# Up-projections of three feed-forward stages as seven products of summed quarters, down-projections in five interleaved groups

## The chip, the cores and the metric

The kernel runs on one core of a Trainium2 chip. The metric is the device time of one execution in microseconds, the median of several runs. One further execution was taken with the hardware profiler; its span, from the first to the last instruction, and its own time stand below.

## The reference, cut to what matters

All tensors are float32. There are 512 tokens, the model width is 1024, the feed-forward width 2816. A first block (mixer, convolutional feed-forward, gate) is followed by two layers, each of them a feed-forward stage, attention and another feed-forward stage:

```python
def swiglu(h, wg, wu, wd):
    return (jax.nn.silu(h @ wg) * (h @ wu)) @ wd

for i in range(DEPTH_2):          # DEPTH_2 = 2
    x = x + 0.5 * swiglu(rmsnorm_2(x, ffn_norm1[i]), ffn1_wg[i], ffn1_wu[i], ffn1_wd[i])
    h = rmsnorm_2(x, mix_norm[i])
    ...                           # i = 0: sliding-window attention, i = 1: latent attention
    x = x + 0.5 * swiglu(rmsnorm_2(x, ffn_norm2[i]), ffn2_wg[i], ffn2_wu[i], ffn2_wd[i])
```

The change touches three of these four stages: the second of layer 0 (f20 below), the first of layer 1 (f11) and the second of layer 1 (f21). f20 and f11 follow each other directly.

## The kernel before

Activations lie transposed: the residual x is eight tiles of 128 features by 512 tokens. Every float32 number that goes into TensorE is split into a high part, rounded to the type fp32r, and the rest; `mm` then makes three matmuls of one product: high by high, high by rest, rest by high. Weights come from one flat array, in the order of their use, in chunks of 128 by 1024 (eight blocks of 128 by 128). `Weights` loads a chunk (tile `wr`), rounds it on ScalarE (`wh`) and subtracts on VectorE (`wl`), up to four chunks ahead.

A stage (`ffn`, `swiglu`, `up_down`) works in this order. Of the 22 blocks of 128 hidden features, twelve are made by `pair(j)`: one chunk for the gate and one for the up-projection, each eight blocks of `mm` into one PSUM bank (24 matmuls of 512 columns), multiplied by the token norms `rB` on VectorE, SiLU on ScalarE, the product of both, and its split. Then `down(0)` sums eleven hidden blocks into each of the eight output tiles and adds them to x. Ten more pairs follow, and `down(1)`. Before a stage's first product can be scaled, `operands` splits x times its gain, and `rstd_tok` and `bcast` make the norms.

The order of instructions on every engine isn't the program's text: calls are recorded by `Order`, and `arrange` lays them out ahead of time by costs, due times and free buffers. A buffer pool has a fixed number of slots; PSUM has five banks for `ps` and three for `pt`. All recorded instructions come out of one line (`Order.emit`), which is why every row of the profile has the same line number.

Of the kernel before, what the change touches and what calls it, by code (L numbers as in the profile page):

```python
# [20 lines left out]
P = 128  # L21
S = 512
D = 1024
KD = D // P
# [5 lines left out]
CH = 1024  # L30
AHEAD = 3
# [7 lines left out]
FEED = (3, 3) + (2,) * 9 + (0,) * 5  # L39
AHEAD_OF = 200  # L40
URGENCY = (0.0, 0.5)
SPARE = {"f": 3, "ps": 3, "e": 2}

# [90 lines left out]
def pack_ffn(which, i):  # L134
    def f(a):
        return pack_up_down(a[f"ffn{which}_wg_2"][i], a[f"ffn{which}_wu_2"][i], a[f"ffn{which}_wd_2"][i])
    return f


def pack_out(w):  # L140
# [230 lines left out]
class Order:  # L371
# [137 lines left out]
    def _arrange(self, strict):  # L509
# [28 lines left out]
        def fits(o):  # L538
# [112 lines left out]

class Weights:
    def __init__(self, nc, pool, flat, sizes):
        self.nc, self.pool, self.flat, self.sizes = nc, pool, flat, sizes
        self.off = 0
        self.made = 0
        self.used = 0
        self.ready = {}

    def _make(self, parts=1):  # L660
        nc, i = self.nc, self.made
        n = self.sizes[i]
        raw = self.pool.tile([P, CH], F32, name="wr", tag="wr", bufs=3)[:, :n]
        h = self.pool.tile([P, CH], F32R, name="wh", tag="wh", bufs=AHEAD + 1)[:, :n]
        lo = self.pool.tile([P, CH], F32R, name="wl", tag="wl", bufs=AHEAD + 1)[:, :n]
        src = self.flat[self.off:self.off + P * n].rearrange("(p n) -> p n", p=P)
        def piece(c):
            nc.sync.dma_start(out=raw[:, c], in_=src[:, c])
            nc.scalar.copy(out=h[:, c], in_=raw[:, c])
            nc.vector.tensor_tensor(out=lo[:, c], in0=raw[:, c], in1=h[:, c].bitcast(F32), op=ALU.subtract)  # L670

        step = n // parts
        todo = [lambda o=o: piece(slice(o, o + step)) for o in range(0, n, step)]
        self.ready[i] = (h, lo)
        self.off += P * n
        self.made += 1
        return todo


    def first(self):  # L680
        return self._make(4)

    def next(self, n):
        while self.made < len(self.sizes) and self.made <= self.used + AHEAD:
            for piece in self._make():
                piece()
        assert self.sizes[self.used] == n, (self.used, self.sizes[self.used], n)
        r = self.ready.pop(self.used)
        self.used += 1
        return r  # L690


class Core:
    def __init__(self, ctx, tc, A, sizes, vo, co):
        self.tc, self.A = tc, A
        self.nc = nc = Order(tc.nc)

        def pool(name, bufs, space=None):
            kw = {} if space is None else {"space": space}
            return LazyPool(ctx.enter_context(tc.tile_pool(name=name, bufs=bufs, **kw)), bufs, space)  # L700

        self.cp = pool("c", 1)
        self.xp = pool("x", 1)
        self.wp = pool("w", 1)
# [11 lines left out]
        self.W = Weights(nc, self.wp, A["w"], sizes)  # L716
        self.bg = []

    def start(self, x_in):
# [24 lines left out]
    def f(self, n=S):  # L744
        return self.fp.tile([P, FW], F32, name="f", tag="f", bufs=12)[:, :n]
# [32 lines left out]
                self.bg.pop(0)()  # L778


    def mm(self, ps, w, x, start, stop):
        te = self.nc.tensor
        te.matmul(ps, lhsT=w[0], rhs=x[0], start=start, stop=False)
        te.matmul(ps, lhsT=w[0], rhs=x[1], start=False, stop=False)
        te.matmul(ps, lhsT=w[1], rhs=x[0], start=False, stop=stop)

    def proj(self, ops, w, o=0, ps=None):
        ps = ps if ps is not None else self.ps()
# [307 lines left out]
        self.swiglu(xo, rB)  # L1096

    def ffn(self, name):
        xo = self.operands(self.v(name, 0, KD))
        rB = self.bcast(self.rstd_tok())  # L1100
        self.swiglu(xo, rB)

    def swiglu(self, xo, rB):
        nc, W = self.nc, self.W

        def pair(j):
            ps = self.proj(xo, W.next(CH))
            g = self.mul(self.f(), ps, rB)
            nc.scalar.activation(out=g, in_=g, func=AF.Silu)
            ps = self.proj(xo, W.next(CH))  # L1110
            u = self.mul(self.f(), ps, rB)
            self.mul(g, g, u)
            return self.split(g)

        self.up_down(pair, 0.5)

# [556 lines left out]
    (pack_ffn(2, 0), lambda c: c.ffn("f20")),  # L1673
    (pack_ffn(1, 1), lambda c: c.ffn("f11")),
    (pack_attn_b, lambda c: c.attn_b()),
    (pack_ffn(2, 1), lambda c: c.ffn("f21")),
]


def layout(a, phases):  # L1680
    vo, vec = pack_vecs(a)
    co, con = pack_consts()
    arrays = pack_misc(a)
    chunks = [ch for pk, _ in phases for ch in pk(a)]
    arrays["vec"] = np.ascontiguousarray(vec)
    arrays["con"] = con
    flat = np.empty(sum(ch.size for ch in chunks), np.float32)
# [5 lines left out]
    return arrays, vo, co, [ch.shape[1] for ch in chunks]  # L1693


def body(tc, A, phases, sizes, vo, co):
# [27 lines left out]
```

## Time and profile before

| | |
|---|---|
| median of 3 runs | 2680.9 us (2680.84 to 2681.42) |
| profiled execution | 2680.98 us, span 2679.2 us |
| mean granted TensorE clock | 0.995 |
| busy: TensorE / weight loads / VectorE / ScalarE | 2653.8 / 2173.9 / 1529.4 / 957.5 us |

Busy time is the union of an engine's instruction intervals. A matmul's interval is longer than its turn on TensorE, because matmuls are pipelined, so the rate is read from the distance between the starts of matmuls that follow each other. A row of VectorE or ScalarE also lasts a little longer than the distance to the next one's start.

### The profile page before, as it was taken

The numbers are of one execution on the slowest core, as the hardware profiler recorded it, in microseconds if no ns is written. First come the engines' busy times: TensorE is split into PE (matmuls) and PEld (weight loads), VectorE is DVE, ScalarE is ACT, GpSimd is POOL, SyncE is SP. The second block draws the span as 40 slices with busy tenths as digits, with TensorE's granted clock in tenths as the row PEclk, the third lists the DMA queues.
The fourth block names the chain that finished last, engine by engine and source line by source line (L and its number), as shares of the span: only waits on it lengthen the run. The fifth ranks groups of instructions, "written<-read, shape, count | busy, mean of one in ns | idle before, by whom it ended". The sixth has DMA issues, their size and how long they took to land. (4 is left out here: it accounts for less than half of the span.)

```text
span 2679.2 us, 32322 instructions
## 1 busy us (share of the span) xinstructions
PE 2653.8 (99%) x12788; PEld 2173.9 (81%) x12788; DVE 1529.4 (57%) x2665; ACT 957.5 (36%) x1487; POOL 120.8 (5%) x193
## 2 busy tenths in 40 slices
PE   9999999999999999999999999999999899999999
PEld 7888888888887888889788888888888766788887
DVE  7526469969858654447664344544344776644342
ACT  4333244323444222235543223322223574432231
POOL 1100000000000000002300000000000142000000
PEclk9999999999999999999999999999999999999999
DMA  5322232333323422324132222222232100323222
GB/s 173 102 95 87 95 100 95 111 117 106 111 92 96 118 95 96 101 87 131 56 107 99 98 95 97 98 97 94 95 102 91 54 17 28 99 94 99 98 94 79
DMA packets 103015, 254.28 MB, mean 95 GB/s; under 512 B 37376, under 2 KB 39296, under 8 KB 102864
## 3 DMA queue, kind: packets, MB, share of 16 engines
q1 hardware_dynamic: 102560, 251.31, 29.0%
q8 instruction: 100, 1.64, 0.2%
q0 software_dynamic: 304, 0.92, 0.1%
q14 instruction: 51, 0.42, 0.0%
HBM read 242.76 MB, written 9.44 MB: 94 GB/s over the span
## 5 line engine op out<-in xcount | busy, mean ns | idle before, releaser
L646 PE MATMUL ps<-op,wh 128*128 128x512 f32 x6624 | 2053.1, 391 | 6.2 <-DVE f L646 3.5
L646 PEld LDWEIGHTS ps<-op,wh 128*128 128x128 f32 x6624 | 1241.6, 188 | 268.5 <-issue 8.1
L646 PE MATMUL ps<-op,wl 128*128 128x512 f32 x3312 | 1292.5, 390 | 0.0
L646 ACT CAST wh<-wr 128x1024 fp32r<-128x1024 f32 (+3 forms) x471 | 469.0, 996 | 1204.6 <-PE ps L646 741.2
L646 PEld LDWEIGHTS ps<-op,wl 128*128 128x128 f32 x3312 | 622.5, 188 | 130.4 <-issue 0.9
L646 DVE TENSOR_TENSOR wl<-wr,wh 128x1024 fp32r<-128x1024 f32 (+3 forms) x471 | 547.2, 1163 | 308.5 <-ACT wh L646 306.6
L646 DVE TENSOR_TENSOR f<-ps,f 128x512 f32<-128x512 f32 x260 | 178.9, 690 | 434.9 <-PE ps L646 431.4
L646 ACT CAST op<-f 128x512 fp32r<-128x512 f32 x136 | 84.2, 621 | 227.4 <-DVE f L646 227.1
L646 DVE TENSOR_TENSOR f<-f 128x512 f32<-128x512 f32 x213 | 147.3, 692 | 27.6 <-ACT f L646 21.4
L646 PE MATMUL ps<-wh,op 128*128 128x256 f32 (+3 forms) x608 | 149.7, 333 | 4.1 <-ACT opf L646 3.4
L646 DVE TENSOR_TENSOR op<-f,op 128x512 fp32r<-128x512 f32 x136 | 93.7, 691 | 67.1 <-ACT op L646 67.0
L646 PEld LDWEIGHTS ps<-wh,op 128*128 128x128 f32 x608 | 105.9, 194 | 12.5 <-ACT opf L646 3.7
L646 ACT ACTIVATE f<-f 128x512 f32<-128x512 f32 x142 | 89.1, 627 | 45.4 <-DVE f L646 45.3
L646 PE MATMUL ps<-wl,op 128*128 128x256 f32 (+3 forms) x304 | 100.1, 329 | 0.0
L646 DVE SCALAR_TENSOR_TENSOR x<-ps,x 128x512 f32<-128x512 f32 (+1 forms) x68 | 44.4, 657 | 93.3 <-PE ps L646 93.3
L646 ACT ACTIVATE f<-x 128x512 f32<-128x512 f32 x80 | 49.3, 628 | 78.1 <-DVE x L646 77.9
L646 DVE TENSOR_TENSOR x<-ps,x 128x512 f32<-128x512 f32 (+1 forms) x57 | 38.7, 680 | 53.8 <-PE ps L646 53.8
L646 DVE SCALAR_TENSOR_TENSOR f<-f,vec 128x512 f32<-128x512 f32 x88 | 64.7, 747 | 1.1 <-ACT f L646 0.9
L646 PEld LDWEIGHTS ps<-wl,op 128*128 128x128 f32 x304 | 58.9, 194 | 3.2 <-issue 0.2
L646 PE MATMUL pt<-con,opf 128*128 128x128 f32 (+1 forms) x348 | 52.9, 279 | 4.2 <-POOL opf L646 2.1
L646 DVE SCALAR_TENSOR_TENSOR op<-x,vec,op 128x512 fp32r<-128x512 f32 x64 | 47.7, 749 | 9.9 <-ACT op L646 9.9
L646 PEld LDWEIGHTS pt<-con,opf 128*128 128x128 f32 (+1 forms) x348 | 38.5, 135 | 16.6 <-issue 4.8
(181 smaller groups left out, 1277.9 us busy)
## 6 DMA issues: line engine op xcount, KB each, us to landing
wr<-in_w SPq DMA_DIRECT2D x411, 512.0 KB, 3.3
wr<-in_w SPq DMA_DIRECT2D x40, 256.0 KB, 2.6
bias<-e SPq DMA_DIRECT2D x28, 256.0 KB, 3.3
opf<-bias SPq DMA_DIRECT2D x16, 448.0 KB, 6.4
x<-in_xT SPq DMA_DIRECT2D x8, 256.0 KB, 4.7
out_y<-x SPq DMA_DIRECT2D x7, 256.0 KB, 2.0
wr<-in_w SPq DMA_DIRECT2D x4, 416.0 KB, 3.1
wr<-in_w SPq DMA_DIRECT2D x12, 128.0 KB, 2.0
```

Of the source, the lines that this page charges most:

```text
L646: getattr(getattr(self.nc, o.eng), o.name)(*[real(a) for a in o.args], **{k: real(v) for k, v in o.kw.items()})
```

## The change

In the three stages, four of the 22 hidden blocks are still made by pairs. The other eighteen are made two at a time, in nine calls of `block(j)`. The weights of two hidden blocks (gate and up, 512 output features) times 1024 input features by 512 tokens are cut into two halves in every direction, and the four quarter products are formed out of seven products of sums of quarters. A product has half the input blocks (four), two of the four feature blocks, and 256 tokens: 24 matmuls of 256 columns into the halves of one PSUM bank. Sums of products that several results share are left in the bank and the next product is added on top (banks b1, b0, b2); what has to be added besides is added by VectorE. The sums of weight quarters (`_sums`) are made on VectorE from the loaded chunks, and all seven are split as other weights are. The sums of activation quarters (`halves`) are made once a stage. `down` no longer runs twice over eleven hidden blocks, but five times over groups of 4, 4, 4, 4 and 6, in parts of four output tiles that stand between the blocks. Weight tiles share one pool of 34 slots with the operands, where there were 22 for operands and eleven for weights.

```diff
+GROUPS = [range(0, 4), range(4, 8), range(8, 12), range(12, 16), range(16, 22)]
...
+def fast_order():
+    out = [("down", 0, range(0, 4))]
+    for g in range(1, len(GROUPS)):
+        js = list(GROUPS[g][::2])
+        if g == 1:
+            out += [("block", js[0]), ("down", 0, range(4, 8)), ("block", js[1])]
+            continue
+        for n, j in enumerate(js):
+            out.append(("block", j))
+            if n < 2:
+                out.append(("down", g - 1, range(4 * n, 4 * n + 4)))
+    return out + [("down", len(GROUPS) - 1, range(0, 8))]
...
+        def s2():
+            st["21"], st["22"] = self._load(CH), self._load(CH)
+            st["s1"] = self._tile("ws", CH)
+            nc.vector.tensor_tensor(out=st["s1"], in0=st["21"], in1=st["22"], op=ALU.add)
+            st["11"] = self._load(CH)
+            st["s2"] = self._tile("ws", CH)
+            minus(st["s2"], st["s1"], st["11"])
+            return self._split(st["s2"])
...
+        def s3():
+            minus(st["21"], st["11"], st["21"])
+            return self._split(st["21"])
...
+        def s4():
+            minus(st["s2"], st["12"], st["s2"])
+            return self._split(st["s2"])
+
+        return [s2, a11, s3, s1, a12, a22, s4]
...
-        self.opp = pool("op", 22)
+        self.opp = pool("op", 34)
...
+    def halves(self, gain, rB):
...
+        for k in range(4):
+            X = self.opf().rearrange("p (a n) -> p a n", a=2)
+            for a in range(2):
+                j = k + 4 * a
+                nc.vector.scalar_tensor_tensor(out=X[:, a], in0=self.x[j], scalar=gain[:, j:j + 1], in1=rB,
+                                               op0=ALU.mult, op1=ALU.mult)
...
+            part(X[:, :, :H], t[:, 0], t[:, 1])
...
+            part(X[:, 1, H:], last[:, k % 2, 0], last[:, k % 2, 1])
...
+            nc.vector.tensor_tensor(out=T[:, 0:2], in0=X[:, :, H:], in1=X[:, 0].rearrange("p (a n) -> p a n", a=2),
+                                    op=ALU.subtract)
+            nc.vector.tensor_tensor(out=T[:, 2], in0=X[:, 1, H:], in1=T[:, 0], op=ALU.subtract)
+            nc.vector.tensor_tensor(out=T[:, 3], in0=X[:, 1, :H], in1=T[:, 2], op=ALU.subtract)
...
+            part(T, h, lo)
...
+        def block(j):
+            def prod(ps, right, start=False):
+                w = W.next(CH)
+                for a in range(2):
+                    for k in range(4):
+                        self.mm(ps[:, a * H:(a + 1) * H], self.wsl(w, a * 512 + k * P, P), B[right][k],
+                                start and a == k == 0, k == 3,
+                                skip_group_check=True)
...
+            b1, b0, b2 = self.ps(), self.ps(), self.ps()
+            prod(b1, "t2", start=True)
+            prod(b0, "b11", start=True)
+            p1 = self.f()
+            nc.scalar.copy(out=p1, in_=b0)
+            prod(b2, "t3", start=True)
+            u2 = plus(self.f(), b1, p1)
+            prod(b1, "t1")
+            u4 = plus(self.f(), b1, p1)
+            low = self.opf()
+            plus(low[:, S:], b2, u4)
+            prod(b0, "b21")
+            prod(b2, "t4")
+            plus(low[:, :S], b2, u2)
+            prod(b1, "b22")
+            c12 = plus(self.f(), b1, p1)
...
```

Three places show what `arrange` makes of it. The rows are in the order of an engine's queue; names carry buffer numbers, and a row ends with the engines or DMA queues whose semaphores it waits for. `op` is an operand's high and rest, `th` and `tl` are those of a sum of activation quarters, `bb` those of a plain quarter, `ws` a sum of weight quarters.

The first place is TensorE in the middle of stage f20. Before, at the passage from one bank to the next:

```order
L646 MATMUL ps_11713<-op_11351,wl_11612 128x512
L646 MATMUL ps_11713<-op_11373,wh_11603 128x512 x2
L646 MATMUL ps_11713<-op_11373,wl_11612 128x512
L646 MATMUL ps_11747<-op_11195,wh_11640 128x512 [waits Activation_49]
L646 MATMUL ps_11747<-op_11195,wh_11640 128x512
L646 MATMUL ps_11747<-op_11195,wl_11649 128x512 [waits DVE_49]
```

Now, in block 10, where the product into b2 (`ps_12729`) ends and the second product into b1 (`ps_12670`) begins:

```order
L691 MATMUL ps_12729<-th_11683,wh_12630 128x256
L691 MATMUL ps_12729<-tl_11693,wh_12630 128x256
L691 MATMUL ps_12729<-th_11683,wl_12640 128x256
L691 MATMUL ps_12670<-th_11523,wh_12642 128x256 [waits DVE_49]
L691 MATMUL ps_12670<-tl_11532,wh_12642 128x256
L691 MATMUL ps_12670<-th_11523,wl_12649 128x256
```

The matmuls are half as wide, and the first one into b1 waits for VectorE, which must have read b1.

The second place is VectorE in the same stage. Before, the six rows of one pair and the next pair's first:

```order
L646 TENSOR_TENSOR f_11715<-ps_11676,f_11441 128x512 [waits PE_49]
L646 TENSOR_TENSOR wl_11720<-wr_11620,wh_11711 128x1024 [waits DMAHW3_49,Activation_49]
L646 TENSOR_TENSOR f_11749<-ps_11713,f_11441 128x512 [waits PE_49]
L646 TENSOR_TENSOR wl_11754<-wr_11657,wh_11745 128x1024 [waits DMAHW4_49,Activation_49]
L646 TENSOR_TENSOR f_11715<-f_11715,f_11749 128x512 [waits DVE_49]
L646 TENSOR_TENSOR op_11767<-f_11715,op_11767 128x512 [waits Activation_49]
L646 TENSOR_TENSOR f_11786<-ps_11747,f_11441 128x512 [waits PE_49]
```

Now, in block 10, the last split of its weights, then u2 (`f_12741`), u4 (`f_12794`) and the lower results (`opf_12802`), with the next weights and their first sums among them:

```order
L691 TENSOR_TENSOR wl_12710<-ws_12548,wh_12699 128x1024 [waits DVE_49,Activation_49]
L691 TENSOR_TENSOR f_12741<-ps_12670,f_12734 128x512 [waits Activation_49]
L691 TENSOR_TENSOR f_12794<-ps_12670,f_12734 128x512 [waits PE_49]
L691 TENSOR_TENSOR opf_12802<-ps_12729,f_12794 128x512 [waits DVE_49]
L691 TENSOR_TENSOR wl_12809<-wr_12731,wh_12788 128x1024 [waits DMAHW5_49,Activation_49]
L691 TENSOR_TENSOR wl_12823<-wr_12760,wh_12811 128x1024 [waits DMAHW6_49,DVE_49,Activation_49]
L691 TENSOR_TENSOR ws_12836<-wr_12763,wr_12791 128x1024 [waits DMAHW7_49,DMAHW0_49,PE_49]
L691 TENSOR_TENSOR f_12828<-f_12828,ps_12702 128x256 [waits Activation_49]
L691 TENSOR_TENSOR opf_12802<-ps_12729,f_12741 128x512 [waits PE_49]
L691 TENSOR_TENSOR f_12866<-f_12866,opf_12802 128x512 [waits Activation_49]
L691 TENSOR_TENSOR ws_12880<-ws_12836,wr_12838 128x1024 [waits DMAHW1_49]
L691 TENSOR_TENSOR wr_12763<-wr_12838,wr_12763 128x1024
```

For a block, seven weight splits and four weight sums now stand in VectorE's queue among the additions that a later product waits for; the last of the block's own splits (`wl_12710`) stands ahead of u2.

The third place is VectorE at the beginning of f20, now, where the last pairs are finished, the first weight sums are made and the first block's products become possible:

```order
L691 TENSOR_TENSOR tl_11693<-tt_11658,th_11683 128x1024 [waits PE_49,Activation_49]
L691 TENSOR_TENSOR op_11697<-f_11546,op_11697 128x512 [waits Activation_49]
L691 TENSOR_TENSOR op_11702<-f_11620,op_11702 128x512 [waits Activation_49]
L691 TENSOR_TENSOR wl_11712<-wr_11391,wh_11464 128x1024 [waits DMAHW0_49,PE_49]
L691 TENSOR_TENSOR f_11719<-ps_11654,f_11458 128x512
L691 TENSOR_TENSOR ws_11727<-wr_11395,wr_11397 128x1024 [waits DMAHW2_49,DMAHW1_49,PE_49]
L691 TENSOR_TENSOR ws_11738<-ws_11727,wr_11399 128x1024 [waits DMAHW3_49,DVE_49,PE_49]
L691 TENSOR_TENSOR f_11750<-ps_11695,f_11458 128x512 [waits PE_49]
L691 TENSOR_TENSOR wr_11395<-wr_11399,wr_11395 128x1024
L691 TENSOR_TENSOR f_11719<-f_11719,f_11750 128x512 [waits DVE_49,Activation_49]
L691 TENSOR_TENSOR wl_11767<-ws_11738,wh_11754 128x1024 [waits Activation_49]
```

Nothing of this stood here before: the last activation sum (`tl_11693`), two sums and a difference of weight quarters, and the split of the first of them (`wl_11767`), for which the first block's first product waits.

## Rows read from the trace of the kernel before

**Rows 1.** The page: span, busy times, engines and clock in 40 slices.

```profile
span 2679.2 us, 32322 instructions
...
PE 2653.8 (99%) x12788; PEld 2173.9 (81%) x12788; DVE 1529.4 (57%) x2665; ACT 957.5 (36%) x1487; POOL 120.8 (5%) x193
```

**Rows 2.** Busy time and granted clock in stages f20, f11 and f21.

```profile
core 0: us, PE busy (x) PEld busy (x) DVE busy (x) ACT busy (x) POOL busy (x), PEclk, DMA share, GB/s
1369.18:1730.34 361.16, 361.13 (x1595) 298.49 (x1594) 164.41 (x204) 106.67 (x129) 0.00 (x0) 1.00 0.30 98
1730.34:2091.37 361.03, 361.03 (x1595) 298.49 (x1594) 162.72 (x202) 104.64 (x127) 0.00 (x0) 1.00 0.29 94
2313.88:2675.26 361.38, 361.38 (x1595) 298.32 (x1593) 152.30 (x188) 94.85 (x112) 0.00 (x0) 1.00 0.29 94
```

**Rows 3.** Waits in stage f20: who for whom, us in total, times, longest.

```profile
ACT wh L646 <- PE ps L646: 101.8, 36, 4.4
DVE f L646 <- PE ps L646: 101.7, 43, 3.4
...
PEld ps L646 <- issue: 0.5, 2, 0.2
```

**Rows 4.** Timeline of f20, TensorE: start us, duration us; 18 matmuls apart.

```profile
1520.00 0.39 PE L646 MATMUL ps<-op,wl 128*128 128x512 f32 x1
...
1524.08 0.39 PE L646 MATMUL ps<-op,wl 128*128 128x512 f32 x1
```

**Rows 5.** Timeline of the sliding-window attention, TensorE: 138 matmuls apart.

```profile
1212.78 0.40 PE L646 MATMUL ps<-wh,op 128*128 128x256 f32 x2
...
1229.34 0.29 PE L646 MATMUL ps<-wh,op 128*128 128x256 f32 x1
```

**Rows 6.** Groups by shape, 1212.4 to 1229.4 us: count, busy us, mean ns.

```profile
L646 PE MATMUL ps<-wh,op 128*128 128x256 f32 x94 | 17.2, 284 | 0.0
L646 PEld LDWEIGHTS ps<-wh,op 128*128 128x128 f32 x93 | 14.5, 192 | 0.0
L646 PE MATMUL ps<-wl,op 128*128 128x256 f32 x47 | 13.4, 285 | 0.0
```

**Rows 7.** Groups by shape in f20, 1400 to 1700 us.

```profile
L646 DVE TENSOR_TENSOR wl<-wr,wh 128x1024 fp32r<-128x1024 f32 x56 | 68.6, 1225 | 46.6 <-ACT wh L646 46.6
L646 ACT CAST wh<-wr 128x1024 fp32r<-128x1024 f32 x55 | 57.9, 1053 | 168.8 <-PE ps L646 89.3 <-issue 79.5
L646 DVE TENSOR_TENSOR f<-ps,f 128x512 f32<-128x512 f32 x39 | 27.0, 692 | 93.4 <-PE ps L646 93.4
L646 ACT ACTIVATE f<-f 128x512 f32<-128x512 f32 x20 | 12.5, 625 | 0.0
L646 DVE SCALAR_TENSOR_TENSOR x<-ps,x 128x512 f32<-128x512 f32 x11 | 7.6, 688 | 11.9 <-PE ps L646 11.9
```

**Rows 8.** Groups by shape over the span: VectorE and ScalarE, other shapes.

```profile
L646 DVE SCALAR_TENSOR_TENSOR f<-f,vec 128x512 f32<-128x512 f32 x88 | 64.7, 747 | 1.1 <-ACT f L646 0.9
L646 DVE TENSOR_TENSOR wl<-wr,wh 128x256 fp32r<-128x256 f32 x12 | 5.0, 421 | 2.8 <-ACT wh L646 2.8
...
L646 ACT COPY f<-ps 128x512 f32<-128x512 f32 x8 | 4.6, 577 | 0.0
L646 ACT CAST wh<-wr 128x256 fp32r<-128x256 f32 x12 | 4.7, 393 | 4.7 <-issue 3.2 <-DMA wr<-in_w 0.8 <-PE ps L646 0.6
```

**Rows 9.** Timeline of f20: VectorE's first product, and how work is handed over.

```profile
1379.33 0.69 DVE L646 TENSOR_TENSOR f<-ps,f 128x512 f32<-128x512 f32 x1 [0.84 <-ACT f L646]
...
1383.29 1.23 DVE L646 TENSOR_TENSOR wl<-wr,wh 128x1024 fp32r<-128x1024 f32 x1 [0.21 <-ACT wh L646]
1384.43 0.69 DVE L646 TENSOR_TENSOR f<-f 128x512 f32<-128x512 f32 x1
...
1392.84 0.39 PE L646 MATMUL ps<-op,wl 128*128 128x512 f32 x1
...
1393.08 1.05 ACT L646 CAST wh<-wr 128x1024 fp32r<-128x1024 f32 x1 [3.86 <-issue]
1393.26 0.69 DVE L646 TENSOR_TENSOR f<-ps,f 128x512 f32<-128x512 f32 x1 [3.31 <-PE ps L646]
...
1394.17 1.23 DVE L646 TENSOR_TENSOR wl<-wr,wh 128x1024 fp32r<-128x1024 f32 x1 [0.21 <-ACT wh L646]
```

**Rows 10.** TensorE in the attention ahead of f20: waits, then the granted clock.

```profile
1265.94 0.33 PE L646 MATMUL pt<-con,opf 128*128 128x128 f32 x1 [0.98 <-POOL opf L646]
1267.36 0.96 PE L646 MATMUL pt<-con,opf 128*128 128x128 f32 x6 [1.09 <-POOL opf L646]
...
1264.00:1268.00 4.00, 1.93 (x16) 1.00 0.04 11
1268.02:1274.84 6.82, 5.94 (x18) 0.50 0.19 56
```

More of the change, by code (lines that the diff above doesn't have):

```diff
@@ L137, in pack_ffn, with pack_fast, f, down @@
     return f
+GROUPS = [range(0, 4), range(4, 8), range(8, 12), range(12, 16), range(16, 22)]
+def pack_fast(which, i):
+    def f(a):
+        wg, wu, wd = (a[f"ffn{which}_w{c}_2"][i] for c in "gud")
+        out = []
+        def block(j):
+            out.append([_cat([b for w in (wg, wu) for b in _blocks(w, range(4 * half, 4 * half + 4), t * P, (t + 1) * P)])
+                        for t, half in ((j + 1, 0), (j + 1, 1), (j, 0), (j, 1))])
+        def down(g, ms):
+            bl = [b for m in ms for b in _blocks(wd, GROUPS[g], m * P, (m + 1) * P)]
+            for n in range(0, len(bl), 8):
+                out.append(_cat(bl[n:n + 8]))
+        for j in GROUPS[0]:
+            for w in (wg, wu):
+                out.append(_cat(_blocks(w, range(KD), j * P, (j + 1) * P)))
+        for step in fast_order():
+            if step[0] == "block":
+                block(step[1])
+            else:
+                down(step[1], step[2])
+        return out
+    return f
+def fast_order():
[10 more added lines that the diff above has]
+    return out + [("down", len(GROUPS) - 1, range(0, 8))]
 def pack_out(w):
@@ L653, in __init__ @@
     def __init__(self, nc, pool, flat, sizes):
-        self.nc, self.pool, self.flat, self.sizes = nc, pool, flat, sizes
+        self.nc, self.pool, self.flat = nc, pool, flat
         self.off = 0
-        self.made = 0
         self.used = 0
[L658 to L666, printed above, removed]
-        def piece(c):
[L668 to L677, printed above, removed]
@@ L680, in first @@
-    def first(self):
-        return self._make(4)
-    def next(self, n):
[L684 to L689, printed above, removed]
+        self.todo = []
+        for n in sizes:
+            if n:
+                self.todo.append((n, lambda n=n: self._split(self._load(n))))
+            else:
+                self.todo += [(CH, f) for f in self._sums()]
@@ new lines, in __init__, with _tile, _from, _load @@
+        self.ready = []
+    def _tile(self, name, n, dt=F32):
+        return self.pool.tile([P, CH], dt, name=name, tag="op")[:, :n]
+    def _from(self, n):
+        self.off += P * n
+        return self.flat[self.off - P * n:self.off].rearrange("(p n) -> p n", p=P)
+    def _load(self, n):
+        raw = self._tile("wr", n)
+        self.nc.sync.dma_start(out=raw, in_=self._from(n))
+        return raw
+    def _split(self, raw):
+        n = raw.shape[1]
+        h, lo = self._tile("wh", n, F32R), self._tile("wl", n, F32R)
+        self._parts(raw, h, lo)
+        return h, lo
@@ new lines, in _parts, with _sums, minus, a11 @@
+    def _parts(self, raw, h, lo):
+        self.nc.scalar.copy(out=h, in_=raw)
+        self.nc.vector.tensor_tensor(out=lo, in0=raw, in1=h.bitcast(F32), op=ALU.subtract)
+    def _sums(self):
+        nc, st = self.nc, {}
+        def minus(out, a, b):
+            nc.vector.tensor_tensor(out=out, in0=a, in1=b, op=ALU.subtract)
+        def s2():
[6 more added lines that the diff above has]
+            return self._split(st["s2"])
+        def a11():
+            return self._split(st["11"])
+        def s3():
+            minus(st["21"], st["11"], st["21"])
+            return self._split(st["21"])
+        def s1():
+            return self._split(st["s1"])
+        def a12():
+            st["12"] = self._load(CH)
+            return self._split(st["12"])
+        def a22():
+            return self._split(st["22"])
+        def s4():
+            minus(st["s2"], st["12"], st["s2"])
+            return self._split(st["s2"])
+        return [s2, a11, s3, s1, a12, a22, s4]
@@ new lines, in first @@
+    def first(self):
+        n, _ = self.todo.pop(0)
+        raw, h, lo = self._tile("wr", n), self._tile("wh", n, F32R), self._tile("wl", n, F32R)
+        src = self._from(n)
+        self.ready.append((n, (h, lo)))
+        def piece(c):
+            self.nc.sync.dma_start(out=raw[:, c], in_=src[:, c])
+            self._parts(raw[:, c], h[:, c], lo[:, c])
+        return [lambda o=o: piece(slice(o, o + n // 4)) for o in range(0, n, n // 4)]
+    def next(self, n):
+        while self.todo and len(self.ready) <= AHEAD:
+            m, f = self.todo.pop(0)
+            self.ready.append((m, f()))
+        m, r = self.ready.pop(0)
+        assert m == n, (m, n)
@@ L778, in step, with mm @@
                 self.bg.pop(0)()
[L781 removed]
+    def mm(self, ps, w, x, start, stop, **kw):
         te = self.nc.tensor
[L783 to L785 removed]
+        te.matmul(ps, lhsT=w[0], rhs=x[0], start=start, stop=False, **kw)
+        te.matmul(ps, lhsT=w[0], rhs=x[1], start=False, stop=False, **kw)
+        te.matmul(ps, lhsT=w[1], rhs=x[0], start=False, stop=stop, **kw)
     def proj(self, ops, w, o=0, ps=None):
@@ L1098, in ffn @@
     def ffn(self, name):
-        xo = self.operands(self.v(name, 0, KD))
+        gain = self.v(name, 0, KD)
+        xo = self.operands(gain)
         rB = self.bcast(self.rstd_tok())
-        self.swiglu(xo, rB)
+        self.fast_swiglu(xo, gain, rB)
     def swiglu(self, xo, rB):
@@ new lines, in fast_swiglu, with pair, block, plus @@
+    def fast_swiglu(self, xo, gain, rB):
+        nc, W = self.nc, self.W
+        H = S // 2
+        hid = {}
+        def pair(j):
+            ps = self.proj(xo, W.next(CH))
+            g = self.mul(self.f(), ps, rB)
+            nc.scalar.activation(out=g, in_=g, func=AF.Silu)
+            ps = self.proj(xo, W.next(CH))
+            u = self.mul(self.f(), ps, rB)
+            self.mul(g, g, u)
+            hid[j] = self.split(g)
+        for j in GROUPS[0]:
+            pair(j)
+            if j == 0:
+                B = self.halves(gain, rB)
+        def block(j):
+            def prod(ps, right, start=False):
[5 more added lines that the diff above has]
+                                skip_group_check=True)
+            def plus(out, a, b):
+                nc.vector.tensor_tensor(out=out, in0=a, in1=b, op=ALU.add)
+                return out
+            b1, b0, b2 = self.ps(), self.ps(), self.ps()
[14 more added lines that the diff above has]
+            c12 = plus(self.f(), b1, p1)
+            up = self.f()
+            for n, c in enumerate((b0, c12)):
+                o = up[:, n * H:(n + 1) * H]
+                nc.scalar.activation(out=o, in_=c[:, :H], func=AF.Silu)
+                self.mul(o, o, c[:, H:])
+            low = low.rearrange("p (n a t) -> p n a t", n=2, a=2)
+            dn = self.f()
+            d3 = dn.rearrange("p (n t) -> p n t", n=2)
+            nc.scalar.activation(out=d3, in_=low[:, :, 0], func=AF.Silu)
+            self.mul(d3, d3, low[:, :, 1])
+            hid[j], hid[j + 1] = self.split(up), self.split(dn)
+        def down(g, ms):
+            n, w, left = 0, None, len(ms) * len(GROUPS[g])
+            for m in ms:
+                ps = self.pt()
+                for j in GROUPS[g]:
+                    if n % 8 == 0:
+                        w = W.next(min(8, left) * P)
+                        left -= 8
+                    self.mm(ps, self.wsl(w, (n % 8) * P, P), hid[j], j == GROUPS[g][0], j == GROUPS[g][-1])
+                    n += 1
+                step = H if g == len(GROUPS) - 1 and m == KD - 1 else S
+                for o in range(0, S, step):
+                    x = self.x[m][:, o:o + step]
+                    nc.vector.scalar_tensor_tensor(out=x, in0=ps[:, o:o + step], scalar=0.5, in1=x,
+                                                   op0=ALU.mult, op1=ALU.add)
+        for step in fast_order():
+            {"block": block, "down": down}[step[0]](*step[1:])
@@ L1672 @@
     (pack_attn_a, lambda c: c.attn_a()),
-    (pack_ffn(2, 0), lambda c: c.ffn("f20")),
-    (pack_ffn(1, 1), lambda c: c.ffn("f11")),
+    (pack_fast(2, 0), lambda c: c.ffn("f20")),
+    (pack_fast(1, 1), lambda c: c.ffn("f11")),
     (pack_attn_b, lambda c: c.attn_b()),
-    (pack_ffn(2, 1), lambda c: c.ffn("f21")),
+    (pack_fast(2, 1), lambda c: c.ffn("f21")),
 ]
@@ L1686, in layout @@
     arrays["con"] = con
+    sizes = [0 if isinstance(ch, list) else ch.shape[1] for ch in chunks]
+    chunks = [c for ch in chunks for c in (ch if isinstance(ch, list) else [ch])]
     flat = np.empty(sum(ch.size for ch in chunks), np.float32)
@@ L1692, in layout @@
     arrays["w"] = flat
-    return arrays, vo, co, [ch.shape[1] for ch in chunks]
+    return arrays, vo, co, sizes
 def body(tc, A, phases, sizes, vo, co):
```

24 lines of the change are left out of this document (21 added, 3 removed).

## The prediction

> **What bounds the kernel now.** I read the page first. TensorE is busy for 2653.8 of 2679.2 us, VectorE for 57% and ScalarE for 36% [rows 1]; a matmul's interval is longer than its turn, so this alone proves nothing. Then the windows of the three stages that the change touches: TensorE is never idle for more than 0.03 us in a stage of 361 us, the granted clock is 1.00 (2.4 GHz), VectorE is busy for 152 to 164 us and ScalarE for 95 to 107 us [rows 2]. The waits say the same from the other side: VectorE and ScalarE wait for TensorE, some 100 us each in f20, while TensorE's weight loads for these banks wait twice, 0.5 us in all [rows 3]. So in these stages time is the number of matmuls times the distance between their starts. That distance comes from the timeline: 18 matmuls of 512 columns in 1524.08 - 1520.00 = 4.08 us, 0.2267 us each [rows 4]. A stage has 1584 of them (22 x 2 x 24 up, 8 x 22 x 3 down), 359.1 us; the remaining 2 us of its window are the token norms and short hand-overs at its head.
>
> **What a product of 256 columns costs.** The change needs matmuls of 256 columns, and the kernel before has a run of them in its attention: 138 in 1229.34 - 1212.78 = 16.56 us, 0.1200 us each [rows 5], of the same types, each with its own weight load of 128x128, which takes 192 ns and is still hidden [rows 6]. The two distances make a straight line, 0.4167 ns a column and 13.3 ns a matmul. So half a matmul costs more than half: this is the term that speaks against the change, and it is already in the 0.1200.
>
> [...]
>
> **The change, part by part.**
>
> *Products.* Two pairs took 4 x 24 = 96 matmuls of 512 columns, 96 x 0.2267 = 21.76 us. A block takes 7 x 24 = 168 of 256 columns, 168 x 0.1200 = 20.16 us. That saves 1.60 us (2.56 us of columns less 0.96 us for 72 more matmuls). Nine blocks in three stages, 27 x 1.60 = 43.2 us. The down-projections keep their 528 matmuls a stage in any grouping, no gain and no loss on TensorE.
>
> *VectorE, steady.* Durations are those of [rows 7, 8]. Two pairs took 4 splits at 1.225, four products with rB and four others at 0.692, 10.4 us. A block takes 11 instructions of 1024 columns (7 splits, 4 sums), 13.5 us; five additions from PSUM, one product and two splits of 512 columns, 5.5 us; two products of 256 at 0.421: 19.9 us under 20.16 us of TensorE. Where a `down` part of four tiles follows (48 matmuls, 10.9 us), two splits and four additions to x, 5.2 us, come along: 25.1 of 31.0 us. Rows overlap a little (a 1.23 us split is followed 1.14 us later [rows 9]), so a block's true load is nearer 18 us. Only blocks 6 and 8 stand next to each other without `down`. Over a stage: 164 now, 9 x 9.5 more for blocks, 24 more additions to x at 0.688 (16.5), `halves` 4 x 5.4 = 21.5: some 287 of 347 us. VectorE is no longer idle half the time, but doesn't become the bound.
>
> *ScalarE.* A block: seven casts at 1.053, a copy from PSUM 0.577, SiLU and casts of 512 at 0.625 three times, two SiLU of 256 at 0.393, 10.6 us of 20.16. Hidden. DMA: the same bytes; its share of 0.3 in these stages [rows 2] goes to 0.31. The sums need three chunks before the first product of a block; they are loaded in the time of the block before.
>
> *Hand-overs inside a block.* Each bank is used again. The second product into b1 waits for u2, that for p1, that for b0's first product; one product (24 x 0.120 = 2.88 us) lies between. From the last matmul's start: its interval of 0.28 us, 0.03 us to the next engine [rows 6, 9], p1 0.58, u2 0.69, 0.04 each to hand over: 1.66 us. TensorE gets there 0.12 + 2.88 = 3.00 us after the same start. Slack 1.34 us. The second product into b2 waits for u4 and the lower half's addition, 1.77 us of 3.00: slack 1.23 us. If a cast of 1.05 us and a split of 1.23 us have each just begun, the first place is late by 0.9 us; the second by nothing. So the loss lies between 0 and 27 x 0.9 = 24 us. In the order of block 10 the last split ahead of u2 can begin when b1's first product has ended, 2.88 us ahead of p1, and u4 follows u2 directly: nothing stands in the way. I take 2 us over all, near the lower end, and keep 24 for the range.
>
> *The head of a stage.* The first product needs every `halves` and the first weight sum. On VectorE, from its first product with rB to that split, 52 instructions: 9 of 1024 columns (11.0 us), 8 scaled by the gain at 0.747 (6.0), 23 of 512 (15.9), 12 of 256 (5.1): 38.0 us. VectorE's first product began 10.15 us after the stage [rows 2, 9]. TensorE has four pairs and 36 matmuls of `down` first, 228 x 0.2267 = 51.7 us, so 41.5 us remain. It fits with 3.5 us to spare. I cost it at nothing; without that cover each stage would lose what is missing.
>
> *Pools.* One pool of 34 slots instead of 22 and 11 lets the other six phases' order shift. They hold TensorE's whole idle time, 25.4 us [rows 1]. A gain is bounded by that; a loss I can't bound from the trace and take as 10 us at most. I take 0.
>
> **Sum.** The profiled execution took 2680.98 us, 1.8 more than its span, and the median is 2680.9. 2680.9 - 43.2 + 2 = 2639.7, say 2640.
>
> **The rivals.**
>
> *Hand-overs take part of it back.* Waits of some 0.5 us in each block, 13 us, give 2651; at the bound of 0.9 us, 2662. For it: VectorE's load in a block is close to TensorE's, and its queue can't be overtaken. Against: the slack above.
>
> *The other phases' order moves the time.* Between 2614 (all idle time there gone) and 2650 (10 us lost). Against a large effect: their work is unchanged.
>
> *The added matmuls cost only their columns.* If the 13.3 ns a matmul were hidden in the new products, a block would save the 2.56 us of columns, 69 us over all, and the time would be 2614. Against: 138 matmuls of the same width in a row at 120.0 ns [rows 5]. [...]
>
> *Slower: the clock falls.* In the attention ahead of f20, TensorE waited 0.98 and 1.09 us within 2 us, and the granted clock then was 0.50 (1.2 GHz) for 6.82 us [rows 10]. Under full load that stretch costs 3.4 us. If the waits at b1 and b2 came near a microsecond, a block could lose 0.9 + 3.4 = 4.3 us against a gain of 1.6; from 10 of the 27 blocks on the gain is gone, and at 14 of them the time is 2640 - 2 + 60 = 2698, say 2700. Against: 0.9 us is the bound for one wait a block, and the pairs' own changes of bank cost nothing here. [...] This trace goes round its banks too, and the clock stays at 1.00 in all three stages.
>
> **How the numbers follow.** My forecast (2634 to 2648) gets 0.60; hand-overs taking part 0.18 (2648 to 2664, its end at 2672); other phases 0.09; columns only 0.03; the slower case 0.06; no change, from several bounds together, 0.04. The range 2630 to 2662 holds the first and most of the second and third. A change of 0.2%, about 5.4 us, is what a measurement of this kernel tells from none. Faster 0.90, the same 0.04, slower 0.06.
>
> **What would show it.** Right: TensorE's windows of f20, f11 and f21 near 347 us each, matmuls of 256 columns 0.120 us apart, clock 1.00, VectorE busy for about 285 us a stage, and no wait of TensorE longer than 0.3 us inside blocks. Wrong in size: waits of `ps` for VectorE at the second product into b1 or b2, or several microseconds at a stage's first product. Wrong altogether: a distance above 0.1295 us (21.76 / 168), where the products save nothing, or granted clocks of 0.50 inside the stages.

## The result, and the profile after

The changed kernel takes **2632.74 us** (median of four runs, 2632.25 to 2633.84) where the kernel before, on the same chip, takes 2680.87: a ratio of 0.9823, with a 95% interval of 0.9808 to 0.9839. The forecast was 2640 in a range of 2630 to 2662, so the sign and the range held, and the middle was 7 us too high.

The page of the kernel after, to be read against [rows 1]: 1944 more matmuls are in the program, TensorE's busy time fell by 48.3 us all the same, and VectorE gained 317 us.

```profile
span 2630.5 us, 36927 instructions
...
PE 2605.5 (99%) x14732; PEld 2225.9 (85%) x14732; DVE 1846.0 (70%) x3076; ACT 1072.0 (41%) x1658; POOL 126.3 (5%) x193
```

The windows of stages f20, f11 and f21 of the kernel after, with the columns of [rows 2] (start:end, length, busy time of each engine, granted clock, DMA share):

```profile
1360.93:1709.46 348.53, 347.36 (x2243) 317.70 (x2242) 270.04 (x339) 146.52 (x185) 0.00 (x0) 1.00 0.30 100
1709.46:2057.98 348.52, 347.36 (x2244) 317.65 (x2243) 267.93 (x339) 143.40 (x184) 0.00 (x0) 1.00 0.27 92
2277.98:2626.51 348.53, 347.44 (x2243) 317.41 (x2241) 254.57 (x320) 131.56 (x165) 0.00 (x0) 1.00 0.26 88
```

Each stage is 12.5 to 12.9 us shorter than in [rows 2]; the three together went from 1083.57 to 1045.58 us, 38.0 less. TensorE now has 1.1 us without work in each, where it had none, and the clock stays at 1.00. VectorE is busy for 255 to 270 us, 17 to 32 less than forecast.

One block of f20, TensorE's rows in the timeline of the kernel after, from its first matmul to the `down` part that follows (a row with x2 is two matmuls run together):

```profile
1501.34 0.28 PE L691 MATMUL ps<-th,wh 128*128 128x256 f32 x1
...
1504.10 0.28 PE L691 MATMUL ps<-th,wl 128*128 128x256 f32 x1
1504.22 0.40 PE L691 MATMUL ps<-bb,wh 128*128 128x256 f32 x2
...
1521.38 0.28 PE L691 MATMUL ps<-bb,wl 128*128 128x256 f32 x1
1521.50 0.63 PE L691 MATMUL pt<-op,wh 128*128 128x512 f32 x2
```

The block takes 1521.50 - 1501.34 = 20.16 us for 168 matmuls, 0.1200 us each, as forecast from [rows 5]: the seven products and their six changes of bank run without a gap.

The stages account for 38.0 of the 48.7 us that the span lost. The rest lies where the change touches no computation. Windows of the kernel before, outside the three stages (start to the first attention, that attention to f20, the second attention to f21):

```profile
0.00:1192.80 1192.80, 1183.83 (x5798) 973.33 (x5799) 773.55 (x1265) 422.98 (x553) 20.61 (x23) 1.00 0.33 105
1192.80:1369.18 176.38, 172.38 (x1150) 150.39 (x1148) 117.88 (x358) 95.06 (x249) 39.91 (x42) 0.98 0.29 93
2091.37:2313.88 222.51, 214.06 (x1061) 154.89 (x1060) 157.79 (x448) 133.26 (x319) 60.25 (x128) 0.97 0.14 40
```

The same three of the kernel after:

```profile
0.00:1184.98 1184.98, 1179.57 (x5799) 970.45 (x5799) 771.90 (x1269) 424.48 (x557) 23.34 (x23) 1.00 0.33 107
1184.98:1360.93 175.95, 171.45 (x1149) 149.90 (x1148) 119.42 (x360) 93.46 (x249) 39.85 (x42) 0.99 0.32 105
2057.98:2277.98 220.00, 212.26 (x1062) 152.79 (x1061) 161.40 (x449) 132.60 (x319) 63.09 (x128) 0.98 0.16 53
```

They are 7.82, 0.43 and 2.51 us shorter, 10.8 together, with the same matmuls (one record more or less). TensorE's idle time in them fell by 3.8 us. The rest, 7.0 us, is busy time. In these windows the kernel before spends 27.3 us at a granted clock of 0.50 (1.2 GHz; five stretches, one of them in [rows 10]), the kernel after 10.2 us (two stretches). A stretch at half the clock can cost at most half of its length, 8.5 us for the 17.1 that went, but it didn't cost that everywhere. Three stretches of the first window, cut at the same matmuls in both kernels, show it (length, TensorE's busy time and matmuls, granted clock, DMA share and GB/s). Before:

```profile
0.00:75.05 75.05, 70.79 (x300) 0.98 0.48 163
362.88:586.29 223.41, 222.46 (x1201) 1.00 0.33 103
812.09:921.27 109.18, 105.41 (x602) 0.98 0.36 107
```

After:

```profile
0.00:75.22 75.22, 69.92 (x301) 1.00 0.52 188
362.63:584.40 221.77, 221.77 (x1201) 1.00 0.33 100
810.37:913.43 103.06, 103.06 (x601) 1.00 0.34 108
```

The low clock at 8 to 12 us, which only the kernel before has, bought the kernel after nothing: its first 75 us are no shorter. From 363 to 586 us, 1.6 us were gained at full clock. From 812 to 921 us, 6.1 us were gained, of which the clock can account for 1.7 (half of a stretch of 3.4 us). Even if all of the busy time that went in the two attentions (0.9 and 1.8 us) is the clock's, it accounts for only 4.4 of the 10.8 us. The executions of the kernel before also differ among themselves: in the 30 that were timed beside the experiments, those with a mean clock of 0.995 took 2681.8 us on average and those with 0.997 or 0.998 took 2679.6.

The largest single piece, at 855 us, shows how it came. VectorE and TensorE of the kernel before, in the timeline at 849 to 856 us:

```profile
850.53 0.69 DVE L646 TENSOR_TENSOR f<-f 128x512 f32<-128x512 f32 x1 [2.05 <-ACT f L646]
851.14 0.68 DVE L646 TENSOR_TENSOR e<-e,poslo 128x512 f32<-128x512 f32 x1
851.74 0.68 DVE L646 TENSOR_TENSOR e<-poshi 128x512 f32<-128x512 f32 x1
852.35 1.22 DVE L646 TENSOR_TENSOR wl<-wr,wh 128x1024 fp32r<-128x1024 f32 x1
853.48 0.68 DVE L646 TENSOR_TENSOR e<-e,poslo 128x512 f32<-128x512 f32 x1
854.08 2.48 DVE L646 TENSOR_TENSOR f<-ps,f 128x512 f32<-128x512 f32 x4
...
854.91 1.10 PE L646 MATMUL ps<-op,wh 128*128 128x512 f32 x2 [3.46 <-DVE f L646]
```

TensorE waits 3.46 us for the product with the token norms at 854.08, ahead of which a weight split (`wl`) and three rows of the attention's preparation (`e`) stand on VectorE. The clock then is at 0.50 from 855.0 to 858.4 us. In the kernel after, VectorE at the same place:

```profile
845.56 0.69 DVE L691 TENSOR_TENSOR f<-f 128x512 f32<-128x512 f32 x1 [1.30 <-ACT f L691]
846.17 0.68 DVE L691 TENSOR_TENSOR e<-e,poslo 128x512 f32<-128x512 f32 x1
846.77 0.68 DVE L691 TENSOR_TENSOR e<-poshi 128x512 f32<-128x512 f32 x1
847.37 0.69 DVE L691 TENSOR_TENSOR f<-ps,f 128x512 f32<-128x512 f32 x1
```

No weight split stands there, the product begins 1.81 us after `f<-f` where it took 3.55, and both the wait and the stretch at 0.50 are gone. That is 1.7 of the 3.46 us; how the order of TensorE's own matmuls at this place took away the rest isn't worked out here.

### The profile page after: what moved, and what is told of

The parts are those of the page before. It is cut to its first block, busy times and chain, and to the rows that moved or that the text cites. A ratio compares the mean times of both kernels' runs of the same rounds, so it can differ in the third digit from the quotient of the medians.

```text
span 2630.5 us, 36927 instructions
## 1 busy us (share of the span) xinstructions
PE 2605.5 (99%) x14732; PEld 2225.9 (85%) x14732; DVE 1846.0 (70%) x3076; ACT 1072.0 (41%) x1658; POOL 126.3 (5%) x193
## 5 line engine op out<-in xcount | busy, mean ns | idle before, releaser
L691 PE MATMUL ps<-op,wh 128*128 128x512 f32 x3840 | 1194.9, 392 | 3.4 <-ACT wh L691 2.4
L691 PEld LDWEIGHTS ps<-op,wh 128*128 128x128 f32 x3840 | 717.6, 188 | 157.4 <-issue 5.2
L691 PE MATMUL ps<-op,wl 128*128 128x512 f32 x1920 | 749.5, 390 | 0.0
L691 PEld LDWEIGHTS ps<-op,wl 128*128 128x128 f32 x1920 | 360.4, 188 | 76.3 <-issue 1.2
L691 PE MATMUL pt<-op,wh 128*128 128x512 f32 x1056 | 326.3, 391 | 3.4 <-ACT op L691 3.3
L691 PE MATMUL ps<-th,wl 128*128 128x256 f32 x864 | 244.5, 283 | 0.0
L691 PE MATMUL ps<-tl,wh 128*128 128x256 f32 x864 | 244.5, 283 | 0.0
L691 PE MATMUL ps<-th,wh 128*128 128x256 f32 x864 | 244.4, 283 | 0.0
L691 PE MATMUL ps<-bb,wh 128*128 128x256 f32 x1296 | 236.8, 283 | 0.0
L691 PE MATMUL pt<-op,wl 128*128 128x512 f32 x528 | 205.0, 389 | 0.0
```

What stands on the lines that cost most here:

```text
L691: getattr(getattr(self.nc, o.eng), o.name)(*[real(a) for a in o.args], **{k: real(v) for k, v in o.kw.items()})
```

## The experiments

**The shared pool alone.** `e1_pool_only` keeps the change but for the three stages' form.

```
-    self.fast_swiglu(xo, gain, rB)          (pack_fast)
+    self.swiglu(xo, rB)                     (pack_ffn)
```

> The three stages are built as before the change; only the shared pool of 34 slots for weights and operands, with three slots kept back from work that runs ahead, stays. Theory A: the 10.7 us that the changed kernel gained outside the three stages (7.8 us before the sliding-window attention, 0.4 in it, 2.5 in the latent attention) come from this pool; then 2680.9 - 10.7 = 2670 us, with the three stages at 361 us each. Rival B: they come from the new stages' own order around them; then 2681 us.

Measured: 2669.13 us, ratio 0.9956 (0.9943 to 0.9968). The windows of its three stages:

```profile
1358.70:1719.65 360.95, 360.95 (x1595) 298.49 (x1595) 163.18 (x205) 104.36 (x128) 0.00 (x0) 1.00 0.28 97
1719.65:2080.50 360.85, 360.85 (x1595) 298.56 (x1594) 159.00 (x202) 100.57 (x126) 0.00 (x0) 1.00 0.27 92
2299.30:2660.62 361.32, 361.21 (x1595) 298.30 (x1593) 146.63 (x185) 86.96 (x106) 0.00 (x0) 1.00 0.25 88
```

They are as in [rows 2], 0.5 us less in sum; the rest of the gain lies outside. (The profiled execution was the fastest of five, 2666.48 us.) The two places of the first window that the result section shows, 363 to 586 and 812 to 921 us, take 221.77 and 103.06 us here too, as in the changed kernel. So theory A holds, and the new form of the stages is then worth 2669.13 - 2632.74 = 36.4 us, 12.1 a stage.

**Which part of the pool.** `e2_spare_only` is the kernel before with one line of the change; `e10_pool_in_turn` is `e1_pool_only` without that line.

```
-SPARE = {"f": 3, "ps": 3, "e": 2}
+SPARE = {"op": 3, "f": 3, "ps": 3, "e": 2}
```

> The kernel before with one entry more: operand buffers may be given out of turn as long as three stay free. The weight pools stay apart. Theory A1: giving out of turn is what moved the other phases; 2670 us. Rival A2: sharing one pool between weights and operands did it; 2681 us.

> The three stages as before the change and the shared pool of 34 slots, but its slots given strictly in turn. Theory S1: sharing the slots between weights and operands is enough for the gain outside the stages; 2669 us as with the pool alone. Rival S2: it takes both, sharing and giving out of turn; 2680 us or more, since weights that run ahead then queue with operands.

Measured: 2683.66 us for the line alone, ratio 1.0011 (1.0002 to 1.0019), and 2738.36 for the shared pool without it, 1.0213 (1.0198 to 1.0227). The longest waits of TensorE in the latter:

```profile
PE pt L691 <- DVE f L691: 19.4, 6, 4.6
PE ps L691 <- ACT op L691: 8.3, 6, 2.3
```

Neither edit gains by itself. Slots given strictly in turn make a shared pool cost 57 us: each request then waits for the oldest slot, whoever holds it, and 61 us of the span run at 0.50, three stretches of 13.7 us among them, where it was 27.3 in the kernel before. So it takes both edits, as rival S2 had it. That the waits come from slots is argued from the edit, which changes nothing else; I didn't trace each one to its slot. The shared pool also has one slot more than the two pools had together (34 against 33), which no run tests apart.

**Is TensorE the bound inside a block?** `e3_six_products` takes 24 of a block's 168 matmuls away.

```
-            prod(b0, "b21")
-            prod(b2, "t4")
+            prod(b0, "b21", parts=1)
+            prod(b2, "t4", parts=1)
```

> Each block leaves out half of the product with t4 and half of the product with b21, 24 matmuls of 256 columns in all; weights, their sums and all additions stay. Theory A, TensorE bounds the blocks: 27 x 24 x 0.120 = 77.8 us less, 2555 us. Rival C, VectorE is already close to being the bound (19.9 us a block by its rows' durations, some 18 us by their distances, against 17.3 us of TensorE): little of it comes out in blocks 6 and 8, which have no down part between them, and the others wait too; 2590 us or more.

Measured: 2553.47 us, ratio 0.9525 (0.9512 to 0.9538), 79.3 below the changed kernel. 27 x 24 x 0.1200 = 77.8 us: time follows the matmuls, though VectorE had the same work in 17.3 us a block. The other 1.5 us are no more than executions of one kernel differ by (1.6 us for the changed kernel).

**How much room VectorE has.** `e4_four_more_sums` makes one sum of the weights five times, `e5_ten_more_sums` eleven times, so a block has 4 or 10 more instructions of some 1.14 us.

```
+            for _ in range(5):        (11 in the second)
                 nc.vector.tensor_tensor(out=st["s1"], ...)
```

> The sum of the two lower weight quarters is computed five times instead of once, the same result each time: four more VectorE instructions of 1024 columns a block, 4.6 us. Theory A: a block with a down part has VectorE busy for 22.7 + 4.6 = 27.3 us of 31.0, so only blocks 6 and 8 (22.6 against 20.2 us) lose something; 2633 to 2645 us. Rival C, VectorE is the bound or close to it: 27 x 2.4 us or more, 2698 us.

> The same with ten more sums of 1024 columns a block, 11.4 us. Theory A: VectorE now needs 34.1 us for a block with a down part, TensorE 31.0, and 29.4 against 20.2 us in blocks 6 and 8; VectorE becomes the bound and each stage loses 15 to 35 us; 2680 to 2740 us. Rival: the planner hides it all, 2633 us; or, if VectorE was the bound before, 27 x 11.4 us, 2940 us.

Measured: 2635.49 us, ratio 0.9829 (0.9814 to 0.9844), and 2790.06, ratio 1.0405 (1.0388 to 1.0423). Four more a block add 112 us to VectorE's busy time and 2.8 us to the kernel. So theory A holds for four. With ten, TensorE's longest waits are for the weights of the products, rounded on ScalarE (`wh`) and split on VectorE (`wl`), both behind the added sums:

```profile
PE ps L691 <- ACT wh L691: 40.8, 44, 6.4
PE ps L691 <- DVE wl L691: 39.0, 36, 6.5
PE ps L691 <- ACT f L691: 11.1, 17, 0.9
```

and its stage f20:

```profile
1359.81:1762.18 402.37, 369.95 (x2244) 330.70 (x2242) 367.98 (x430) 146.11 (x185) 0.00 (x0) 0.96 0.26 87
```

VectorE is now busy for 91% of the stage. TensorE is idle for 32.4 us of it, and is busy for 22.6 us more than in the changed kernel with the same matmuls, and 34.1 us of the stage run at 0.50. At most half of these, 17.1 us, is the clock's part of the 22.6. The idle time alone lies in the expectation's 15 to 35 us a stage; the whole costs more than its top, since it had left out that the clock falls with the waits.

**The hand-over by itself.** `e6_u2_five_times` makes the sum on which b1's second product waits five times, 2.4 us more than its one time, against a slack worked out as 1.34.

```
+            u2 = self.f()
+            for _ in range(5):
+                plus(u2, b1, p1)
```

> The addition u2, which the second product into bank b1 waits for, is computed five times, the same result each time. The chain from b0's first product becomes 1.66 + 4 x 0.60 = 4.07 us, TensorE gets there after 3.00 us. Theory H, a late hand-over costs TensorE its lateness: 27 x 1.07 = 29 us, 2662 us. Rival P, another product (with b21) is put ahead of the one that waits, or the chain was longer covered than worked out: 2633 to 2637 us.

Measured: 2636.19 us, ratio 0.983 (0.9815 to 0.9844), 3.4 us above the changed kernel; TensorE waits for these sums twice, 2.5 us in all. In the block shown in the result section, 13 of the 24 matmuls of product b21 (into b0) now stand ahead of t1 (into b1): the planner, which goes by costs, fills the gap with another product, as rival P had it. So this run doesn't measure the slack. In the changed kernel it can be read: in the block shown above, u2 is

```profile
1507.91 0.69 DVE L691 TENSOR_TENSOR f<-ps,f 128x512 f32<-128x512 f32 x1 [1.31 <-ACT f L691]
```

and ends at 1508.60 us, and t1 is due at 1501.34 + 3 x 2.88 = 1509.98, 1.38 us later.

**The head of a stage.** `e7_two_pairs` leaves two pairs ahead of the blocks instead of four, and has ten blocks.

```
-GROUPS = [range(0, 4), range(4, 8), range(8, 12), range(12, 16), range(16, 22)]
+GROUPS = [range(0, 2), range(2, 6), range(6, 10), range(10, 16), range(16, 22)]
```

> Two hidden blocks by pairs and twenty by blocks, in groups of 2, 4, 4, 6 and 6. TensorE saves one more block a stage, 3 x 1.60 = 4.8 us. Theory A on a stage's head: the first product has 96 + 24 matmuls of 512 columns ahead of it, 27.2 us, VectorE needs 10.2 us until its first product and then some 28 us for the halves, the pairs and the first weight sum; TensorE waits some 10 us a stage; 2633 - 4.8 + 31 = 2659 us. Rival: the head is not what four pairs are needed for; 2628 us.

Measured: 2641.99 us, ratio 0.9855 (0.984 to 0.987). Its f20 takes 351.99 us, 3.5 more than with four pairs, despite one block more (1.6 us). In the timeline TensorE waits for the operands at the first products and the clock is at 0.50 for 6.8 us from 1389.8:

```profile
1390.00 0.58 PE L691 MATMUL ps<-bb,wh 128*128 128x256 f32 x1 [2.22 <-DVE bb L691]
1391.79 0.58 PE L691 MATMUL ps<-tl,wh 128*128 128x256 f32 x1 [0.25 <-DVE tl L691]
```

The cover is needed, as the expectation had it, but the loss is about 5 us a stage and not 10. TensorE reached the first product 25.7 us after the stage's start instead of 55.0; on VectorE four weight splits and a weight sum stood among the first steps of the norms (1364.47 to 1370.5 us), and seven of the eight `bb` rows, three of them of 512 columns, stood behind that product.

**A fourth stage.** `e8_fourth_stage` gives f10 the same form, and steps the preparation of the attention that runs beside it after each pair and twice after each block; `e9_fourth_stage_later` steps it once after each block only.

```
+            self.step()          (e8: after each pair)
...
+            self.step(2)         (e8; e9: self.step(), after each block)
```

> The first feed-forward stage of layer 0 is done in the same way as the other three, with the preparation for the attentions, which runs beside it, in steps after each pair and two after each block. Theory A: 43.2 / 3 us less the 1.8 us that a stage lost at its head, 12.6 us; 2620 us. Rival C: the preparation for the attentions takes the VectorE time that blocks need there; 2627 to 2633 us.

> As the kernel with four stages done in the new way, but the nine pieces of preparation for the attentions that fall into its first stage stand one behind each block, none beside the pairs at the stage's head. Theory D: in the run before, the VectorE work of these pieces among the sums of activation quarters held back the first block (TensorE waited 11.3 and 7.5 us there, and the granted clock was then 0.50 for 20.5 us); without it the fourth stage gains what the others gained, 12.6 us, 2620 us. Rival R: the stage's longer head (the final norm is applied to x and a second norm computed before the sums can begin) makes the wait; then 2632 to 2640 us again.

Measured: 2638.24 us, ratio 0.984 (0.9825 to 0.9854), and **2626.89, ratio 0.9797 (0.9783 to 0.9811)**, the best of all, 5.9 us under the changed kernel. TensorE at the head of f10, timeline of the first:

```profile
877.21 0.80 PE L691 MATMUL ps<-bb,wh 128*128 128x256 f32 x2 [11.27 <-ACT wh L691]
885.51 0.58 PE L691 MATMUL ps<-th,wh 128*128 128x256 f32 x1 [7.50 <-ACT wh L691]
```

and of the second, the same place:

```profile
854.07 1.22 PE L691 MATMUL ps<-op,wh 128*128 128x512 f32 x2 [2.67 <-DVE f L691]
...
879.74 0.39 PE L691 MATMUL ps<-th,wh 128*128 128x256 f32 x1 [0.59 <-ACT wh L691]
```

In the first, VectorE has the attention's position products among the sums of the operands, and the clock is at 0.50 for 20.5 us from 869.8, round the two waits. With the preparation put behind, most of this goes, but not all: f10 gives about half of the 12.1 us that the other stages give. The first run is slower than both of its expectations; the second lies between theory D and rival R, so the place of the preparation was the larger part of the loss, and what keeps the rest isn't shown. The two ratios' intervals touch (0.9811 and 0.9808), but each of the five executions is faster than each of the changed kernel's four.

## Why the prediction was right, and where it was off

**Products: right.** A block takes the 20.16 us of the sum. The rival in which the added matmuls cost only their columns (2614) falls with it: 168 matmuls at 0.1200 us. The Trainium skill's "TensorE: Matmul & The Clock Gate", section "Back-to-back issue gap", has N / 2.4 + 2.5 ns for a single matmul by itself at full clock, 109 ns at 256 columns; in this stream, where each matmul has its own weight load, the run shows 120.

**Hand-overs inside a block: right, nearly nothing.** TensorE's waits in f20 and f11 of the kernel after are, in full:

```profile
PE pt L691 <- ACT op L691: 2.2, 2, 1.1
```

and f21 has one more of 1.1 us. That is once a stage, at its head; the products of a block never wait for a bank, not even where no `down` stands between two blocks. The slack is 1.38 us where 1.34 was worked out. The 2 us that the sum set down for this place are not found there.

**The head: placed right, costed wrong.** "It fits with 3.5 us to spare" held for the first product: the first weight split ends at 1412.00 us in f20, 51.1 us after the stage's start, and the product starts at 1415.98, 4.0 us later. But it counted VectorE's instructions up to that split, not what else waits in the queue behind one of them. In f20 of the kernel after, the timeline has:

```profile
1409.05 1.22 DVE L691 TENSOR_TENSOR wr<-wr 128x1024 f32<-128x1024 f32 x1
...
1410.15 0.39 PE L691 MATMUL pt<-op,wl 128*128 128x512 f32 x1
1410.18 0.69 DVE L691 TENSOR_TENSOR f<-f 128x512 f32<-128x512 f32 x1
...
1410.95 0.62 ACT L691 CAST op<-f 128x512 fp32r<-128x512 f32 x1 [1.28 <-DVE f L691]
...
1411.62 1.53 PE L691 MATMUL pt<-op,wh 128*128 128x512 f32 x5 [1.09 <-ACT op L691]
...
1412.99 0.40 PE L691 MATMUL pt<-op,wl 128*128 128x512 f32 x1
...
1417.77 0.28 PE L691 MATMUL ps<-th,wh 128*128 128x256 f32 x1
1418.13 0.73 PE L691 MATMUL pt<-op,wh 128*128 128x512 f32 x2
```

and the weight load of the last of these rows:

```profile
1418.13 0.30 PEld L691 LDWEIGHTS pt<-op,wh 128*128 128x128 f32 x2 [0.28 <-DVE x L691]
```

What was late isn't the first product but a `down` matmul ahead of it: the third weight sum (`wr<-wr`), which no product needs yet, stood in front of the last pair's product f, and the cast and the matmul followed. The idle time of 1.09 us is less than what was lost, because a matmul's interval (0.39 us) reaches beyond its turn (0.2267). By the starts, the six matmuls from 1410.15 to 1412.99 took 2.84 us instead of 1.36, 1.5 us more. A second, smaller wait stands inside the first block of f20 and f11, where the planner has put the last 12 of the first `down` part's matmuls: the first of these waits until VectorE's addition to x has freed a bank of `pt`, 0.36 us after the matmul before instead of 0.12, and with the distance behind it some 0.35 us are lost. The sum had 2 us for all that isn't products; it should have been 5.2: the three stages took 1045.58 us, not 1083.57 - 43.2 = 1040.4. Three times 1.5 and twice 0.35 us make up these 5.2. So the hand-over that cost something is one of `down`, at the head, a place that was set at nothing.

**Pools: the term mis-sized.** "I take 0", between a gain of 25.4 and a loss of 10. It was a gain of 10.8 in the changed kernel and 11.7 by itself in `e1_pool_only`. The bound was also too narrow in kind: it counted TensorE's idle time alone, and two thirds of the gain are busy time, in part (some 4.4 us) from stretches at 0.50 that didn't come. The rival that named this had 0.09.

With measured terms: 2680.9 - 43.2 + 5.2 - 10.8 = 2632.1, against 2632.7. The forecast's own range of 2634 to 2648 missed by 1.3 us; the range for all cases held. The middle was off by 7 us and not by 11 because the head's 3.2 us went the other way; that part is luck.

**VectorE's load: 255 to 270 us, forecast about 287.** Adding up durations counts twice where they overlap, as [rows 9] already showed for one split: in f20 of the kernel after they add up to 288 us, and VectorE is busy for 270.

**The slower rival** didn't come here, but `e5_ten_more_sums` shows what it describes: waits inside blocks, with 0.50 about them, 2790 us. The waits there are for weights, not for the sums at b1 and b2 that the rival named. The loss starts somewhere between 4 and 10 more sums a block. The Trainium skill's "TensorE: Matmul & The Clock Gate", section "A second HAM failure mode: psum-queue depth-cycling", tells of a kernel that went round the PSUM banks with idle moments between groups and whose clock went to and fro. In this kernel going round them alone left the clock at 1.00, and so did the waits of 1.1 us at the heads. Inside these stages it fell in `e5_ten_more_sums`, with waits up to 6.5 us, and in `e7_two_pairs`, with waits up to 2.5 us.

## What to carry to other kernels

Where TensorE has no idle time, count matmuls by their measured distance at each width: half a width is not half a price, and the measured price of a run elsewhere in the same kernel carried over to the third digit. Idle time of another engine can pay for fewer products as long as its work between two uses of a bank fits; check the queue's order at the head of the stage instruction by instruction, since a sum can be short enough and still stand in the wrong place. And when a buffer pool is changed, the phases that it doesn't mean to touch have to be costed too, with the stretches of low clock that their waits cause.

## What the runs showed of the hardware

A wait of a few microseconds can cost more than itself. In the kernel before, 3.46 us of waiting at 854.9 us were followed by 3.4 us at 0.50; in `e7_two_pairs`, 6.8 us at 0.50 begin in a wait of 2.2 us; in `e8_fourth_stage`, 20.5 us at 0.50 lie round waits of 11.3 and 7.5 us. In `e5_ten_more_sums` this made at most 17.1 us of a stage's 53.8 us loss. By contrast the stretch at 0.50 from 8 to 12 us in the kernel before made no difference that can be seen, and the 1.1 us waits at the heads in the changed kernel left the clock at 1.00.

Weight loads of 128x128 take 192 ns by their rows and come every 120 ns in the blocks, two under way at a time, with no gap in TensorE's matmuls. Rows of busy time can hide short waits: in f20 a wait of 1.09 us by the intervals was a loss of 1.5 us by the starts.
